# The gate of attention computed with seven products of sums, behind the pooled branch's product

## The chip, the core and the metric

The kernel runs on one core of a Trainium2 chip. A core has engines with instruction queues of their own: TensorE (PE, matrix products; PEld is its weight load), VectorE (DVE), ScalarE (ACT), GpSimd (POOL) and SyncE (SP, which here issues DMAs). They wait for each other by semaphores; each takes its instructions in the order in which they were recorded. The metric is the device time of one execution in microseconds (us), lower is better.

## The reference

Two layers of the same kind over T = 528 tokens (16 learned meta tokens and 512 of the input), width 1024. Cut to what matters here:

```python
h = rms_norm(x, norm_g)
q, k, v, gate_a, u_b, gate_b, q_idx, k_idx, w_idx, merge = split(h @ w_in)
score = einsum(relu(q_idx . k_idx), w_idx)        # per query, over visible keys
_, sel = top_k(score, 128)                        # 128 keys per query
attn = softmax_attention(q, k[sel], v[sel])       # 8 heads of 64
y_a = (attn * silu(gate_a)) @ w_a                 # gate_a: 512 columns
pooled = multiscale_pool(u_b, pool_w, pool_b, pool_s)
y_b = (pooled * silu(gate_b)) @ w_b
g_a, g_b = split(sigmoid(merge))                  # 2 x 1024 columns
out = x + (g_a * y_a + g_b * y_b) @ w_out
```

`k_top` is min(256, 512 // 4) = 128, so a query tile needs 16 rounds of "the eight largest, then strike them out".

## The kernel before

**Numbers.** Every matrix product is made of three of the fast format fp32r: each operand is split into a high part (rounded to fp32r) and a low part (what is left), and high x high, high x low and low x high are summed in PSUM. `hhi` and `hlo` are the parts of h, transposed: 8 blocks of 128 rows by 528 tokens.

**Weights.** All weights pass as a list of chunks of 128 x 2048 numbers, in the order of use (L112 to L124). `w_load` (L129) fetches a chunk into `raw` over SP's queue. `w_prep_enqueue` (L155) then puts the items of its preparation into `prep_q`, one chunk ahead of use. There are three kinds: plain (ACT makes the high part, DVE the low part), `by_dma` (ACT makes the high part and a negated copy, to which an accumulating DMA on POOL's queue adds the raw weights, L189 to L199), and `mixed` (L212 to L277). The mixed kind serves a scheme in which a 2 x 2 block product is made from seven products of sums of blocks instead of eight: nine items, in which ACT casts seven blocks and DVE makes seven low parts and five sums of weight blocks, each 128 x 512.

**The two ways to multiply.** `dense` (L495) computes 128 output columns for up to 512 tokens: 24 matmuls for 8 blocks of depth. `mix_gates` (L878) computes a chunk of 256 output columns for all tokens in two halves of `n2` (264 in layer 0, 256 in layer 1) as seven products of twelve matmuls, named "a11", "a12", "s2", "s1", "s3", "s4" and "a22". The sums of h that it needs (`hsum`) are made by `sums_of_h` (L806) during earlier stages, part of them by way of DRAM (`far`, `hsheet`). Three PSUM banks U, S and X change roles by chunk (`ROLES`, L875). `total` adds a partial result out of PSUM on DVE, `gate` applies tanh on ACT (sigmoid and silu are made of tanh). Ahead of a product the items of preparation that it needs are recorded (`NEEDS`), and after each product more of them, `LEAD` = 5 items ahead.

**The stages of a layer**, in PE's order: keys and index queries; the pooled branch's gate (dense); the pooled branch's input (dense); queries of heads 0 to 3; *the attention gate, two dense chunks, into* `sila`; queries of heads 4 to 7; y_b = the pooled branch's product with `w_b`, two chunks, into `zb`; the merge gates, eight chunks with `mix_gates`; y_a, the product with `w_a`; the output product.

**What is woven in between.** After each group of matmuls `group_done` (L320) runs work that is due, in this order: functions put off by `later`; an item of `prep_q`; steps of the generator at the head of `fill` (the attention), at `rate` steps per group, half of that in `half_done`; and steps of the top-k:

```python
spare[0] += FULL * (pe.us - seen[0]) - (dve.us - seen[1])
spare[0] = min(spare[0], CAP)
while spare[0] > 0 and sel:
    next(sel[0])                      # one step; its DVE cost is taken off spare
```

`pe.us` and `dve.us` are sums of costs that the code itself assigns to the instructions recorded so far (`pe_cost`, `dve_cost`, L71 and L80: a fp32r matmul costs n / 2167 us, a DVE operation 0.15 us and 0.00104 us a column). `topk_steps` (L635) serves two query tiles at once: a step is a pair of MAX8 or a pair of MATCH_REPLACE8, 16 rounds of two steps each. Query tiles 0 and 1 go first, then tiles 2 and 3, whose rows have 400 and 528 keys.

The attention (L657) goes through 16 units u of two heads (u // 4 is the query tile), with three steps each. In step one of unit u the logits of u + 1 and the scaling of u, in step two the softmax of u + 1 and the values of u - 1, in step three the transposes of u and, behind each tile, `gated` (L744): the tile's result times `sila`, in place. Before a tile's first logits, `ensure(i)` in `attend` (L1141) finishes the top-k that the tile needs: for tiles 0 and 1 the first generator, for tiles 2 and 3 both, recording all that is left at once. `splits` and `alos` then make the parts `ahi` and `alo` for y_a. The attention is put into `fill` ahead of y_b (L1153), at R_ATT = 1.95 (layer 0) and 1.7 (layer 1).

Of the kernel before, what the change touches and what calls it, by code (L numbers as in the profile page):

```python
# [26 lines left out]
HB = 272  # L27
NCOL = 968
LB = 6
R_ATT = (1.95, 1.7)  # L30
FULL = 1.0
CAP = 1.5
W0 = 3
# [54 lines left out]
def tile_block(ctx: ExitStack, tc: tile.TileContext, x, meta, w_in, pool_w, w_a, w_b, w_out, rows, hgain, c_tab, out):  # L88
# [24 lines left out]
    for l in range(2):  # L113
        wi = w_rows(w_in[l], 0, w_in.shape[2])
        chunks.append([(wi[:, :, 512:640], 0), (wi[:, :, 2688:2816], 128)])
        mb = [3784, 4040, 4296, 4552]
        order = [2176, 2432, 1664, 1920, 1408, 1152, 0, 640, 896, 256]
        chunks += [[(wi[:, :, c:c + 256], 0)] for c in order]
        chunks += [[(w_rows(w_b[l], c, 512), 0)] for c in (0, 512)]
        by_dma |= set(range(len(chunks) - 10, len(chunks)))  # L120
        mixed |= set(range(len(chunks), len(chunks) + 8))
        chunks += [[(wi[:, :, c:c + 256], 0)] for c in (*mb, 2760, 3016, 3272, 3528)]
        chunks += [[(w_rows(w_a[l], c, 512), 0)] for c in (0, 512)]
        chunks += [[(w_rows(w_out[l], c, 256), 0)] for c in (0, 256, 512, 768)]  # L124

# [171 lines left out]
    def later(fn, n=2):  # L297
        pend.append((count[0] + n, fn))
# [358 lines left out]
    def attention(ensure):  # L657
# [92 lines left out]
        for u in range(-1, 17):  # L750
            if u + 1 < 16:
                logits(u + 1)
            if 0 <= u < 16:
                scale(u)
            yield
            if u + 1 < 16:
                soft(u + 1)
            if u >= 1:
                values(u - 1)
                if u % 4 == 0:  # L760
                    meta_values(u // 4 - 1)
            yield
            if u >= 1 and u % 4 == 0:
                gated(u // 4 - 1)
            if 0 <= u < 16:
                turn(u)
                if u % 4 == 3:
                    meta_turn(u // 4)
            yield
# [36 lines left out]
    def sums_of_h(l, s0, n2):  # L806

        ts_ = one.tile([128, 2, 2, 4, T // 2], F32R, tag="R", name="hsum")
        c0, c1 = slice(s0, s0 + n2), slice(s0 + n2, s0 + 2 * n2)
        far = dram.tile([128, 2, 2, 2, n2], F32, name=f"far{l}")  # L810
        nf = NF[0]
        t1_ = []

        def sums(g):
            k = slice(2 * g, 2 * g + 2)
            a0, a1, b0, b1 = nf[0][:, k, c0], nf[0][:, k, c1], nf[1][:, k, c0], nf[1][:, k, c1]
            dve.tensor_tensor(a0, a1, a0, op=OP.subtract)
            dve.tensor_tensor(a1, b1, a1, op=OP.subtract)
            dve.tensor_tensor(b1, b1, a0, op=OP.subtract)
            dma(far[:, 0, g], a0)  # L820
            act.copy(ts_[:, 1, 0, k, :n2], a1)
            act.copy(ts_[:, 0, 0, k, :n2], b1)

        def lows(g):
            k = slice(2 * g, 2 * g + 2)
            a1, b0, b1 = nf[0][:, k, c1], nf[1][:, k, c0], nf[1][:, k, c1]
            dve.tensor_tensor(b0, b0, b1, op=OP.subtract)
            dma(far[:, 1, g], b0)
            dve.tensor_sub(ts_[:, 1, 1, k, :n2], a1, f(ts_[:, 1, 0, k, :n2]))
            dve.tensor_sub(ts_[:, 0, 1, k, :n2], b1, f(ts_[:, 0, 0, k, :n2]))  # L830

        back = {}

        def fetch(w, g):
            if (w, g) == (0, 1):
                back[w, g] = [(slice(k, k + 1), sheet(n2, "hsheet")[:, None, :n2]) for k in (2, 3)]
            else:
                t = tmp.tile([128, T], F32, tag="B", name="hsheet", bufs=8) if w == 0 else sheet(T, "hsheet")
                back[w, g] = [(slice(2 * g, 2 * g + 2), t[:, :2 * n2].rearrange("p (k c) -> p k c", k=2))]
            for k, t in back[w, g]:  # L840
                dma(t, far[:, w, g, k.start - 2 * g:k.stop - 2 * g])

        def high(w, g):
            if w == 0 and not t1_:
                t1_.append(one.tile([128, 2, 4, T // 2], F32R, tag="Alo", name="hsum1"))
            for k, t in back[w, g]:
                act.copy(H[0][:, k, c1] if w else t1_[0][:, 0, k, :n2], t)

        def low(w, g):
            for k, t in back.pop((w, g)):  # L850
                hi, lo = [H[s][:, k, c1] if w else t1_[0][:, s, k, :n2] for s in range(2)]
                dve.tensor_sub(lo, t, f(hi))

        early = deque([lambda: sums(0), lambda: lows(0), lambda: sums(1), lambda: lows(1)])
        late = deque([lambda: fetch(1, 0), lambda: fetch(1, 1), lambda: high(1, 0), lambda: low(1, 0),
                      lambda: high(1, 1), lambda: low(1, 1), lambda: fetch(0, 0), lambda: fetch(0, 1)])

        def last_sum():
            for g in range(2):
                high(0, g)  # L860
            for g in range(2):
                low(0, g)

        operands = {
            "a11": lambda s, k: H[s][:, k, c0],
            "a12": lambda s, k: H[s][:, 4 + k, c0],
            "s4": lambda s, k: H[s][:, 4 + k, c1],
            "s1": lambda s, k: t1_[0][:, s, k, :n2],
            "s2": lambda s, k: ts_[:, 0, s, k, :n2],
            "s3": lambda s, k: ts_[:, 1, s, k, :n2],  # L870
            "a22": lambda s, k: H[s][:, k, c1],
        }
        return early, late, last_sum, operands
# [1 line left out]
    ROLES = [(0, 1, 2), (2, 0, 1), (1, 2, 0)]  # L875
    NEEDS = {"a11": 1, "a12": 2, "s2": 4, "s1": 5, "s3": 6, "s4": 7, "a22": 8}

    def mix_gates(zb, ta, s0, n2, operands, splits, alos):  # L878
        base = popped[0] - progress[W["use"]]
        end_ = [None]  # L880
        for q in range(8):
            c = W["use"]
            W["use"] += 1
            ops = ready[c]
            w_prep_enqueue()
            bs = [bank("d") for _ in range(3)]
            U, S, X = (bs[r] for r in ROLES[q % 3])
            done = [0]

            def product(ps, name, start):  # L890
# [8 lines left out]
            def end():  # L899
                done[0] += 1  # L900
                group_done()
                while prep_q and (popped[0] < base + 9 * q + LEAD + done[0] * 9 // 7 or (q == 7 and done[0] > 4)):
                    prep_one()

            def gate(eh, t, src, in_sheet):
                j = 2 * q + eh
                cs = slice(s0 + t * n2, s0 + (t + 1) * n2)
                if q < 4:
                    th = src if in_sheet else sheet(n2, "th")[:, :n2]
                    act.activation(th, src, AF.Tanh, scale=0.5)  # L910
                    d = zb[:, j, cs]
                    later(lambda: dve.scalar_tensor_tensor(d, th, 1.0, d, op0=OP.add, op1=OP.mult), 2)
                else:
                    end_[0] = act.activation(ta[j - KT][:, cs], src, AF.Tanh, scale=0.5).ins

            def total(eh, t, ps, part):
                o = sheet(n2, "c")[:, :n2]
                dve.tensor_tensor(o, ps[:, :n2], part, op=OP.add)
                gate(eh, t, o, True)

# [30 lines left out]
            end()  # L951
            splits()
            ready.pop(c)
        return end_[0]


# [41 lines left out]
    for l in range(2):  # L998
# [124 lines left out]
        ta = {}  # L1123

        queries(0)
        sa = one.tile([128, 4, T], F32, tag="D", name="sila")
        SIL["a"] = sa
        for c in range(2):
            w = chunk()
            for mi in range(2):  # L1130
                j = 2 * c + mi
                for hf, a, n, o in halves:
                    ps = dense(w, mi, a, n)
                    th = sheet(n, "th")
                    act.activation(th[:, :n], ps[:, :n], AF.Tanh, scale=0.5)
                    later(lambda th=th, ps=ps, j=j, a=a, n=n: dve.scalar_tensor_tensor(
                        sa[:, j, a:a + n], th[:, :n], 1.0, ps[:, :n], op0=OP.add, op1=OP.mult), 1)
                    group_done()
        queries(1)

        def attend():  # L1141
            def ensure(i):
# [7 lines left out]
            if l == 0:  # L1150
                yield from meta_attn(qm)

        fill.append(attend())  # L1153
        rate[0] = R_ATT[l]
        for c in range(2):
            w = chunk()
            if c == 1:
                hold[0] = 5
            for mi in range(4):
                j = 4 * c + mi  # L1160
                for hf, a, n, o in halves:
                    ps = dense(w, mi, a, n, (mhi, mlo), 4)
                    act.copy(zb[:, j, a:a + n], ps[:, :n])  # L1163
                    if late and (l == 1 or hf):
                        late.popleft()()
                    group_done() if hf else half_done()
# [14 lines left out]
                a, n = alo_q.pop(0)  # L1181
                dve.tensor_sub(alo[:, :, a:a + n], sa[:, :, a:a + n], f(ahi[:, :, a:a + n]))

        gates_end = mix_gates(zb, ta, s0, n2, operands, splits, alos)
        drain()
        splits()
        alos()
# [147 lines left out]
```

## Time and profile before

| | us |
|---|---|
| median of 3 runs (lowest, highest) | 772.63 (771.91, 772.87) |
| the profiled execution | 774.25 |
| its span, first to last instruction | 772.5 |
| PE, DVE, ACT, POOL busy in the span | 754.8, 557.9, 475.0, 235.4 |
| mean granted PE clock | 0.991 of full speed |

A row of the profile names the source line (most have L60, the line of the helper that records PE's and DVE's instructions), the engine, the operation and the tiles as out<-in. In a group's row stand the count, the busy time in us, the mean duration in ns, and the idle time of the engine just before with what ended it. A matmul's own duration (about 290 ns) overlaps with those of its neighbours; what one costs PE is read from the time of a series. In a timeline and in the chain of waits the two first numbers are start and duration in us. A wait's row has the sum, the number of times and the longest.

### The profile page before, as it was taken

Reading aid. Unit: us, or ns where it says so; the run is one execution under the profiler, and the core shown is the slowest. Engines: PE = TensorE matmul, PEld = TensorE weight load, DVE = VectorE, ACT = ScalarE, POOL = GpSimd, SP = SyncE. Lnnn points to the kernel's source line nnn. Section 1 sums busy time; section 2 is a strip of 40 time slices with the busy share of each in tenths; the row PEclk is TensorE's granted clock in tenths of the full one; section 3 lists DMA queues with packets and bytes.
Section 4 is the critical chain, followed back from the end, with each engine's and each line's share of the span. In section 5 each row is a group of like instructions: output and inputs, shape, how many; then the busy total and the mean of one; then the engine's idle time right before and its main releaser. Section 6 shows DMA issues by size and latency. Waiting matters only on the chain.

```text
span 772.5 us, 15843 instructions
## 1 busy us (share of the span) xinstructions
PE 754.8 (98%) x5989; PEld 718.7 (93%) x5989; DVE 557.9 (72%) x1396; ACT 475.0 (61%) x1046; POOL 235.4 (30%) x304
## 2 busy tenths in 40 slices
PE   6999999999999999999999999999999999999998
PEld 5999999999999999999999988988979899999998
DVE  6856787888787786775357658868799887769531
ACT  5577754736788786534244787365668887864420
POOL 6552164425220110043345421652511221104300
PEclk8999999999999999999999999999999999999999
DMA  8538586586022111453513477858721221136311
GB/s 294 183 83 217 140 178 165 125 204 165 2 83 83 55 56 56 149 183 115 161 58 109 111 195 173 192 127 205 183 87 56 75 90 56 56 109 221 129 50 42
DMA packets 73549, 96.96 MB, mean 126 GB/s; under 512 B 3664, under 2 KB 58736, under 8 KB 73472
## 3 DMA queue, kind: packets, MB, share of 16 engines
q1 hardware_dynamic: 67712, 74.97, 30.5%
q0 software_dynamic: 5760, 20.97, 14.8%
q8 instruction: 47, 0.77, 0.4%
q14 instruction: 30, 0.25, 0.1%
HBM read 66.41 MB, written 8.55 MB: 97 GB/s over the span
## 4 chain that ended last, share of the span: by engine, by line
PE 82%; DVE 9%; ACT 5%; POOL 1%; issue 1%; DMA 1%; SPq 0%; DVEq 0%; ACTq 0%; POOLq 0%
PE d L60 67%; PE a L60 11%; PE v L60 4%; DVE w L60 2%; DVE nf L60 1%; ACT lt L691 1%; DVE hlo L60 1%; ACT w L222 1%; DVE t L60 1%; DVE sc L60 1%; DMA hsheet<-far 1%; DVE alo L60 0%; DMA xt<-in_x_dram 0%; DVE raw L60 0%; DVE m L60 0%
## 5 line engine op out<-in xcount | busy, mean ns | idle before, releaser
L60 PE MATMUL d<-hhi,w 128*128 128x256 f32 (+3 forms) x1408 | 289.8, 297 | 0.0
L60 PEld LDWEIGHTS d<-hhi,w 128*128 128x128 f32 x1408 | 226.3, 188 | 7.0 <-issue 1.6
L60 PE MATMUL d<-hlo,w 128*128 128x256 f32 (+3 forms) x704 | 193.6, 294 | 0.6 <-POOL hlo L1202 0.6
L60 PE MATMUL d<-w,hhi 128*128 128x256 f32 (+2 forms) x928 | 145.8, 286 | 2.0 <-DVE w L60 0.9
L60 PEld LDWEIGHTS d<-hlo,w 128*128 128x128 f32 x704 | 132.5, 188 | 3.3 <-POOL hlo L1202 0.8
L60 PEld LDWEIGHTS d<-w,hhi 128*128 128x128 f32 (+1 forms) x928 | 125.8, 187 | 6.4 <-ACT hhi L462 2.2
L60 DVE TENSOR_TENSOR w<-raw,w 128x512 fp32r<-128x512 f32 (+1 forms) x130 | 110.0, 857 | 2.2 <-ACT w L222 2.1
L703 POOL TENSOR_SCALAR pm<-lt,rs 128x16 f32<-128x16 f32 x64 | 40.3, 644 | 183.1 <-DVE rs L60 169.2
L60 PE MATMUL d<-w,hlo 128*128 128x256 f32 (+2 forms) x464 | 85.2, 282 | 0.0
L60 PE MATMUL d<-hsum,w 128*128 128x264 f32 (+1 forms) x576 | 77.8, 286 | 0.0
L60 PEld LDWEIGHTS d<-hsum,w 128*128 128x128 f32 x576 | 72.0, 188 | 1.5 <-issue 0.7
L60 PEld LDWEIGHTS d<-w,hlo 128*128 128x128 f32 (+1 forms) x464 | 68.0, 187 | 0.4
L192 POOL DMA_DIRECT2D w<-raw x40 | 36.4, 925 | 104.0 <-ACT w L191 83.4
L222 ACT CAST w<-raw 128x512 fp32r<-128x512 f32 x96 | 56.3, 623 | 2.9 <-DVE raw L60 2.9
L1202 POOL TENSOR_TENSOR hlo<-ta,hhi 128x256 fp32r<-128x256 f32 (+1 forms) x32 | 31.1, 988 | 82.0 <-ACT hhi L1201 82.0
L60 DVE MATCH_REPLACE8 sc<-m,sc 128x400 f32<-128x400 f32 (+2 forms) x100 | 54.3, 548 | 0.0
L60 DVE MAX8 m<-sc 128x8 f32<-128x400 f32 (+2 forms) x100 | 52.7, 556 | 0.8
L691 ACT ACTIVATE lt<-lt,mn,NR 128x144 f32<-128x144 f32 (+3 forms) x64 | 42.4, 665 | 12.0 <-DVE mn L60 12.0
L60 PE MATMUL d<-mhi,w 128*128 128x272 f32 (+2 forms) x192 | 48.9, 331 | 0.4 <-ACT zb L1163 0.4
L191 ACT ACTIVATE w<-raw 128x1024 fp32r<-128x1024 f32 x40 | 41.3, 1057 | 11.3 <-PE d L60 11.3
L60 DVE SCALAR_TENSOR_TENSOR sc<-r,wsg,sc 128x144 f32<-128x144 f32 (+3 forms) x56 | 32.4, 581 | 15.5 <-ACT r L615 13.2
L580 POOL TENSOR_TENSOR t<-t,t 128x256 f32<-128x256 f32 (+1 forms) x34 | 30.8, 907 | 39.2 <-DVE t L60 39.2
(199 smaller groups left out, 1372.4 us busy)
## 6 DMA issues: line engine op xcount, KB each, us to landing
raw<-in_w_in_dram SPq DMA_DIRECT2D x72, 512.0 KB, 3.9
w<-raw POOLq DMA_DIRECT2D x40, 512.0 KB, 5.9
raw<-in_w_out_dram SPq DMA_DIRECT2D x16, 512.0 KB, 3.4
kept<-res SPq DMA_DIRECT2D x16, 264.0 KB, 2.5
res<-kept SPq DMA_DIRECT2D x16, 264.0 KB, 6.5
raw<-in_w_branch_b_dram SPq DMA_DIRECT2D x8, 512.0 KB, 4.4
raw<-in_w_branch_a_dram SPq DMA_DIRECT2D x8, 512.0 KB, 3.5
xt<-in_x_dram SPq DMA_DIRECT2D x4, 512.0 KB, 5.3
```

The source lines that it names most:

```text
L60: return fn(*a, **k)
L191: act.activation(t, raws[c][s], AF.Copy, scale=-1.0)
L192: gp.dma_start(t, raws[c][s], accum_op=OP.add)
L222: act.copy(t[:, 0], blk[src[n]])
L580: gp.tensor_tensor(t1[:m, :256], t1[:m, :256], t2[:m, :256], op=OP.add)
L691: act.activation(L[hh][:, :n], L[hh][:, :n], AF.Exp, scale=NR[:, i, h:h + 1], bias=mn[:, hh:hh + 1], accum_out=sm[:, hh:hh + 1])
L703: gp.tensor_scalar(pms[i][:, 2 * j + hh, :], L[hh][:, 0:16], rs[:, hh:hh + 1], None, op0=OP.mult)
L1202: gp.tensor_sub(hlo[:, j, a:a + n], d, f(hhi[:, j, a:a + n]))
```

## The change

The attention gate's two chunks (columns 640 and 896 of `w_in`) are taken out of the dense stages and put ahead of the merge gates in `mix_gates`, whose loop now runs over q = -2 to 7. The results go to `sila`; the formula is the same (tanh of the half, plus one, times the value). In `chunks` they leave `by_dma` for `mixed`. Queries of heads 4 to 7 follow directly on those of heads 0 to 3. The attention is put into `fill` one chunk later, ahead of y_b's second chunk, with R_ATT = 1.55 and 1.4, and waits before the third step of unit 4, which is the first to use `sila`, until both gate chunks are done (`SIL["ready"]`). One buffer of `hsheet` moves from tag "B" to tag "L" of the pool `tmp`.

```diff
-R_ATT = (1.95, 1.7)
+R_ATT = (1.55, 1.4)
...
-        order = [2176, 2432, 1664, 1920, 1408, 1152, 0, 640, 896, 256]
+        order = [2176, 2432, 1664, 1920, 1408, 1152, 0, 256]
...
-        by_dma |= set(range(len(chunks) - 10, len(chunks)))
-        mixed |= set(range(len(chunks), len(chunks) + 8))
-        chunks += [[(wi[:, :, c:c + 256], 0)] for c in (*mb, 2760, 3016, 3272, 3528)]
+        by_dma |= set(range(len(chunks) - 8, len(chunks)))
+        mixed |= set(range(len(chunks), len(chunks) + 10))
+        chunks += [[(wi[:, :, c:c + 256], 0)] for c in (640, 896, *mb, 2760, 3016, 3272, 3528)]
...
             yield
+            while u == 4 and not SIL["ready"]:
+                yield
             if u >= 1 and u % 4 == 0:
                 gated(u // 4 - 1)
...
-                t = tmp.tile([128, T], F32, tag="B", name="hsheet", bufs=8) if w == 0 else sheet(T, "hsheet")
+                t = sheet(T, "hsheet")
...
-    def mix_gates(zb, ta, s0, n2, operands, splits, alos):
+    def mix_gates(sa, zb, ta, s0, n2, operands, splits, alos):
...
-        for q in range(8):
+        for q in range(-2, 8):
...
-            U, S, X = (bs[r] for r in ROLES[q % 3])
+            U, S, X = (bs[r] for r in ROLES[(q + 2) % 3])
...
-                while prep_q and (popped[0] < base + 9 * q + LEAD + done[0] * 9 // 7 or (q == 7 and done[0] > 4)):
+                while prep_q and (popped[0] < base + 9 * (q + 2) + LEAD + done[0] * 9 // 7 or (q == 7 and done[0] > 4)):
...
-                if q < 4:
+                if q < 0:
+                    th = sheet(n2, "th")[:, :n2]
+                    act.activation(th, src, AF.Tanh, scale=0.5)
+                    d = sa[:, j + 4, cs]
+                    later(lambda: dve.scalar_tensor_tensor(d, th, 1.0, src, op0=OP.add, op1=OP.mult), 1)
+                elif q < 4:
...
-                o = sheet(n2, "c")[:, :n2]
+                cs = slice(s0 + t * n2, s0 + (t + 1) * n2)
+                o = sa[:, 2 * q + eh + 4, cs] if q < 0 else sheet(n2, "c")[:, :n2]
...
             ready.pop(c)
+            SIL["ready"] = q >= -1
...
         queries(0)
+        queries(1)
         sa = one.tile([128, 4, T], F32, tag="D", name="sila")
         SIL["a"] = sa
-        for c in range(2):
-            w = chunk()
-            for mi in range(2):
-                j = 2 * c + mi
-                for hf, a, n, o in halves:
-                    ps = dense(w, mi, a, n)
-                    th = sheet(n, "th")
-                    act.activation(th[:, :n], ps[:, :n], AF.Tanh, scale=0.5)
-                    later(lambda th=th, ps=ps, j=j, a=a, n=n: dve.scalar_tensor_tensor(
-                        sa[:, j, a:a + n], th[:, :n], 1.0, ps[:, :n], op0=OP.add, op1=OP.mult), 1)
-                    group_done()
-        queries(1)
+        SIL["ready"] = False
...
-        fill.append(attend())
         rate[0] = R_ATT[l]
         for c in range(2):
             w = chunk()
             if c == 1:
                 hold[0] = 5
+                fill.append(attend())
```

More of the change, by code (lines that the diff above doesn't have):

```diff
@@ L1182, in alos @@
                 dve.tensor_sub(alo[:, :, a:a + n], sa[:, :, a:a + n], f(ahi[:, :, a:a + n]))
-        gates_end = mix_gates(zb, ta, s0, n2, operands, splits, alos)
+        gates_end = mix_gates(sa, zb, ta, s0, n2, operands, splits, alos)
         drain()
```

## The prediction

> **What bounds the kernel now.** I read the page's busy line first, then the waits of PE over the whole span, then each engine's share by stretch.
>
> ```profile
> PE 754.8 (98%) x5989; PEld 718.7 (93%) x5989; DVE 557.9 (72%) x1396; ACT 475.0 (61%) x1046; POOL 235.4 (30%) x304
> ```
> ```profile
> PE v L60 <- ACT hhi L462: 2.4, 3, 1.1
> PE d L60 <- DVE alo L60: 2.1, 2, 1.8
> ```
> ```profile
> 139.30:163.30 24.00, 24.00 (x202) 24.00 (x202) 22.65 (x62) 13.06 (x22) 6.49 (x7) 1.00 0.74 177
> ...
> 191.00:326.30 135.30, 133.77 (x1138) 127.54 (x1137) 102.68 (x268) 104.29 (x256) 18.29 (x30) 1.00 0.21 66
> ```
>
> PE is the bound: busy 754.8 of 772.5 us, and its two longest waits, summed by releaser, are 2.4 and 2.1 us. The windows' columns are the busy time of PE, PEld, DVE, ACT and POOL, the PE clock, the DMA share and GB/s. The first window is the attention gate's two chunks in layer 0, the second runs from the start of y_b to the end of the merge gates. Less work on PE is therefore worth its full time, as long as DVE keeps up; and under the attention gate DVE was busy 22.65 of 24.00 us. The next view keeps only DVE's work on the top-k maxima (MAX8, MATCH_REPLACE8 and its load), for the attention gate's stretch of either layer.
>
> ```profile
> 139.30:163.30 24.00, 17.06 (x44) 1.00 0.74 177
> ...
> 521.00:543.60 22.60, 13.80 (x36) 1.00 0.89 202
> ```
>
> So the dense gate was the cover of the top-k of query tiles 2 and 3: 17.06 us of it in layer 0, 13.80 us in layer 1.
>
> **PE work removed and added.** The chain of waits shows what a group costs on PE.
>
> ```profile
> 139.33 3.08 PE d L60 x24
> ...
> 142.70 2.92 PE d L60 x24
> ...
> 203.27 0.50 PE a L60 x4
> 203.77 1.43 PE d L60 x12
> 205.20 0.37 PE v L60 x4
> ...
> 258.69 1.46 PE d L60 x12
> ...
> 524.25 2.85 PE d L60 x12
> ...
> 583.00 1.61 PE d L60 x12
> ```
>
> Layer 0 loses four groups of 272 columns and four of 256: 4 x 3.08 + 4 x 2.92 = 24.0 us. Layer 1 loses eight times twelve matmuls of 512 columns: 8 x 2.85 = 22.8 us. Each layer gets 14 products of twelve matmuls: with 264 columns 14 x 1.45 = 20.3 us, with 256 columns (half of 2.85) 14 x 1.42 = 19.9 us. PE saves 3.7 + 2.9 = **6.6 us**. Some products of the mix take 1.61 us, so up to 28 x 0.16 = 4.5 us could be given back; I take 0 and keep 4.5 for the range.
>
> **Weights and sums.** Two chunks per layer leave the route of ACT casts and an accumulating DMA for the mixed one: 12 DVE operations of 512 columns each (7 low parts, 5 sums), and each product chunk has three additions out of PSUM.
>
> ```profile
> L60 DVE TENSOR_TENSOR w<-raw,w 128x512 fp32r<-128x512 f32 x96 | 64.8, 683 | 2.2 <-ACT w L222 2.1
> ...
> L60 DVE TENSOR_TENSOR c<-d,p 128x264 f32<-128x264 f32 x16 | 6.9, 430 | 16.4 <-PE d L60 12.5 <-ACT lt L691 2.2 <-ACT lt L702 1.5
> ```
>
> That is 24 x 0.683 + 6 x 0.43 = 19 us more DVE work per layer, none of it removed elsewhere, beside 20 us more of PE in the same stretch. Over a whole stretch it fits: DVE had 32.6 us of room there (135.30 - 102.68) and gets 20 us of PE time more. Price as an average: 0. The second row says also that DVE, when it reaches an addition, mostly stands waiting for PE (12.5 of 16.4 us idle): it is not behind when the burst below begins. The four accumulating DMAs per layer that go from POOL's queue, the moved loads on SP's queue and ACT's three small copies per chunk lie under a PE that is busy 133.77 of 135.30 us in this stretch: 0 each; the waits quoted name no DMA, and a late load would show there first.
>
> **Where the top-k goes.** This is the main term. A top-k step is issued only while the code's credit is positive: PE's metered cost less DVE's (L331 to L341). In the mix a chunk meters 84 x 264 / 2167 = 10.2 us for PE and, at 12 x 0.68 + 7 x 0.425, 11.1 us for DVE, the attention not counted; the credit has no floor, goes negative, and no step runs. Before, about 15 of the 32 instruction pairs that make up the top-k of tiles 2 and 3 ran under layer 0's dense gate (the 44 above, less a load for each replacement), and the rest beside queries and y_b. In the instruction list of the changed kernel 5 pairs of layer 0 stand ahead of y_b, 14 in it, none beside products 1 to 24; then `ensure(2)` (attention step 25, forced by logits of tile 2, after product 25) empties the generator at once: **13 pairs, 26 instructions in a row on DVE**. In layer 1 it is 5, 12, and then **15 pairs, 30 instructions**, after product 28. What a pair costs back to back, here under the dense gate, and what ends the top-k:
>
> ```profile
> 159.22 1.18 DVE L60 MAX8 m<-sc 128x8 f32<-128x400 f32 x2
> 160.32 0.07 DVE L60 MATCH_VALUE_LOAD sc<-m,sc 128x8 f32 x1
> 160.38 0.56 DVE L60 MATCH_REPLACE8 sc<-m,sc 128x400 f32<-128x400 f32 x1
> 160.86 0.08 DVE L60 MATCH_VALUE_LOAD sc<-m,sc 128x8 f32 x1
> 160.93 0.69 DVE L60 MATCH_REPLACE8 sc<-m,sc 128x528 f32<-128x528 f32 x1
> 161.53 0.43 DVE L60 SCALAR_TENSOR_TENSOR sila<-th,d 128x272 f32<-128x272 f32 x1
> ...
> 208.35 0.70 DVE L60 TENSOR_SCALAR sc<-sc 128x400 f32<-128x400 f32 x2
> ```
>
> A pair of maxima takes 160.32 - 159.22 = 1.10 us, a pair of replacements 161.53 - 160.32 = 1.21 us. Layer 0: 7 x 1.21 + 6 x 1.10 + 0.70 = 15.8 us. Layer 1: 8 x 1.21 + 7 x 1.10 + 0.70 = 18.1 us.
>
> What is queued behind it on DVE: the reciprocal with which the last exponentials are scaled, the low parts of the next weights, the additions that free PSUM. Who waits for that: in layer 0 PE's transposes of tile 1's last pair of heads, which need the scaled exponentials; in layer 1 the product "s2" of the next chunk, which needs its low part. DVE cannot start early either: the last addition before the burst waits for product 23 of PE in layer 0, for product 27 in layer 1. Between that and the wall PE has in layer 0 three products, four matmuls of logits, four of values and four transposes: 3 x 1.45 + 0.50 + 0.37 + 0.50 = 5.7 us; in layer 1 three products, logits, values and two matmuls: 4.3 + 0.50 + 0.37 + 0.24 = 5.4 us. (The logits are of 400 columns; the quoted four are shorter, so 0.2 us more is possible.)
>
> ```profile
> L60 DVE RECIPROCAL rs<-sm 128x2 f32<-128x2 f32 x32 | 5.1, 160 | 9.1 <-ACT lt L691 9.1
> ...
> L702 ACT ACTIVATE lt<-lt,rs 128x256 f32<-128x256 f32 x16 | 7.2, 501 | 0.8 <-DVE rs L60 0.8
> ```
>
> DVE's side in layer 0: addition 0.43, a low part 0.68, burst 15.8, two small operations 0.3, then two scalings on ACT 1.0: 18.2 us, less 5.7: **12.5 us** of PE stall. Layer 1: 0.43 + 18.1 + 0.3 + a low part 0.68 = 19.5, less 5.4: **14.1 us**. Bounds: 11 and 12.5 us if operations in a row overlap more than the rows show; 14 and 16 us if DVE enters the burst up to 2 us late.
>
> **After the stall.** DVE then holds the work that piled up behind the burst, and PE runs for some products at DVE's pace. The trace shows besides what the clock does after an idle PE, at the end of layer 0's merge gates.
>
> ```profile
> 328.00:330.00 2.00, 0.71 (x5) 0.72 (x6) 1.23 (x4) 0.42 (x1) 0.00 (x0) 0.95 0.96 297
> 330.00:332.00 2.00, 2.00 (x11) 2.00 (x11) 0.88 (x2) 0.42 (x1) 0.34 (x1) 0.50 1.03 350
> 332.00:334.00 2.00, 2.00 (x14) 2.00 (x14) 0.85 (x2) 0.32 (x1) 0.42 (x1) 0.70 1.05 407
> ```
> ```profile
> 329.29 0.89 PE L60 MATMUL d<-alo,w 128*128 128x272 f32 x4 [1.85 <-DVE alo L60]
> 329.97 1.91 PE L60 MATMUL d<-ahi,w 128*128 128x256 f32 x8
> 331.68 1.05 PE L60 MATMUL d<-alo,w 128*128 128x256 f32 x4
> 332.53 1.47 PE L60 MATMUL d<-ahi,w 128*128 128x272 f32 x8
> ...
> 334.33 1.11 PE L60 MATMUL d<-ahi,w 128*128 128x256 f32 x8
> ```
>
> After 1.85 us idle the granted clock was 0.50 and 0.70 for about 4 us, and the twelve 256-column matmuls from 329.97 to 332.53 took 2.56 us where twelve take 1.42: some 1.6 us lost with the neighbours. I charge 2.0 us per layer for both effects, 0 if the slow PE only fills DVE's arrears, 3.5 if they add. [...]
>
> **The end of the stage.** In layer 1 the last attention step now falls after the last product, so tile 3 is multiplied, cast and split there.
>
> ```profile
> 696.96 1.29 DVE L60 TENSOR_TENSOR alo<-sila,ahi 128x512 fp32r<-128x512 f32 x2
> 698.16 0.42 DVE L60 TENSOR_TENSOR c<-d,u 128x256 f32<-128x256 f32 x1
> 698.50 1.28 DVE L60 TENSOR_TENSOR alo<-sila,ahi 128x512 fp32r<-128x512 f32 x2
> ```
>
> The second low part that y_a's first group needs moves from ahead of that addition to behind it and behind the multiplication (0.68 us): 1.0 us later. In layer 0 only the 16 meta columns come late: 0.3 us. Together 1.3 us; 0 to 3 for the range.
>
> **Sum.** The profiled execution took 774.25 us, 1.75 around its span of 772.5. 774.25 - 6.6 + 12.5 + 14.1 + 4.0 + 1.3 = 799.6 us; it lay 1.6 us over the median of 772.63, so **798 us**.
>
> **Rivals.**
> *The burst is covered* (faster): PE has enough ahead to run through it. Then 772.63 - 6.6 + 1.3 = 767.3 us. For it: PE busy 133.77 of 135.30 us in the old stretch. Against it: the top-k lay mostly ahead of that stretch, and PE would need 16 us of work between two points that hold 5.7. It decides from there: a burst under 5.7 us costs nothing.
> *DVE never recovers* (slower still): the arrears, at most the 5.7 us that PE ran ahead, delay exponentials and weights up to the end of the attention, and each chunk waits anew. 5 us per layer more, 808 us. Against it: averaged over the stretch DVE has room.
> *The products save nothing*: at 1.61 us they give back 4.5 us: 802 us; a handful in the old mix are so long, most are 1.43 to 1.46.
>
> **How the numbers follow.** Forecast 0.85, never recovers 0.07, products save nothing 0.04, covered 0.04. The low end takes the low bounds (stalls 23.5, arrears 1, tail 0.5: 772.63 - 6.6 + 25 = 791), a little lower for overlap: 789; the high end 772.63 - 6.6 + 30 + 7 + 3 = 806. A time within 0.2% of before is as good as no change here; no case lands there but by cancellation: 0.01. Faster 0.04, slower 0.95.
>
> **What would show it.** In the profile after: about 6.6 us less PE work; on DVE a run of 26 and one of 30 top-k instructions with nothing between; PE idle 12 to 14 us during each, the transposes in layer 0 and a product on "hsum" in layer 1 behind it; a granted clock near half just after; no stall of that size elsewhere. I am wrong if PE works through the burst, or if its stalls lie elsewhere, as in y_b, where DVE also has little room.

## The result, and the profile after

The changed kernel takes **800.73 us** (median of 4 runs, 800.17 to 801.9) against 772.75 for the kernel before (4 runs on the same chip): ratio 1.0352, 95% interval 1.0332 to 1.0373. It is slower by 28 us; 798 was predicted. The profiled execution took 800.17 us with a span of 798.4, so the span grew by 25.9.

From the page after, PE's and DVE's busy time:

```profile
PE 751.4 (94%) x6037; PEld 719.3 (90%) x6037; DVE 590.9 (74%) x1456; ACT 479.5 (60%) x1074; POOL 225.3 (28%) x296
```

PE was busy 98% of the span and is now 94%. DVE has 33.0 us more to do (590.9 - 557.9), 16.5 per layer. The waits of PE after (sum, times, longest):

```profile
PE d L60 <- DVE w L60: 16.9, 4, 15.2
PE a L60 <- ACT lt L702: 12.2, 1, 12.2
PE d L60 <- DVE sila L60: 2.3, 2, 1.2
...
PE d L60 <- DVE alo L60: 1.3, 1, 1.3
```

Before, no sum was above 2.4 us. Two single waits, 12.2 and 15.2 us, come to 27.4 us, more than the span grew; all the rest together is a gain of 1.5. The timeline of DVE after, around the first and then the second of them:

```profile
228.00 0.42 DVE L60 TENSOR_TENSOR c<-d,p 128x264 f32<-128x264 f32 x1
228.34 0.68 DVE L60 TENSOR_TENSOR w<-raw,w 128x512 fp32r<-128x512 f32 x1
228.94 0.08 DVE L60 MATCH_VALUE_LOAD sc<-m,sc 128x8 f32 x1
...
244.01 0.70 DVE L60 TENSOR_SCALAR sc<-sc 128x400 f32<-128x400 f32 x2
...
244.70 0.15 DVE L60 RECIPROCAL rs<-sm 128x2 f32<-128x2 f32 x1
...
620.54 0.42 DVE L60 TENSOR_TENSOR c<-d,u 128x256 f32<-128x256 f32 x1
620.87 0.08 DVE L60 MATCH_VALUE_LOAD sc<-m,sc 128x8 f32 x1
...
638.24 0.70 DVE L60 TENSOR_SCALAR sc<-sc 128x400 f32<-128x400 f32 x2
...
639.00 0.67 DVE L60 TENSOR_TENSOR w<-s,w 128x512 fp32r<-128x512 f32 x1
```

and the timeline of PE after for the same two places (in brackets the idle time before the group and what ended it):

```profile
231.56 1.72 PE L60 MATMUL d<-hsum,w 128*128 128x264 f32 x12
245.51 1.30 PE L60 MATMUL a<-consts,lt 128*128 128x128 f32 x4 [12.22 <-ACT lt L702]
...
624.10 0.40 PE L60 MATMUL d<-hsum,w 128*128 128x256 f32 x2
639.72 2.50 PE L60 MATMUL d<-hsum,w 128*128 128x256 f32 x10 [15.23 <-DVE w L60]
```

This is the burst of the prediction: an addition, in layer 0 one low part, then only top-k from 228.94 to 244.6 us and from 620.87 to 638.8 us. Behind it stand the reciprocal (whose scaling on ACT PE's transposes wait for) and, in layer 1, the low part of a product that PE had begun with two matmuls. The stretches after the stalls, from the windows after (busy PE, PEld, DVE, ACT, POOL, then the granted clock, DMA share and GB/s):

```profile
236.00:240.00 4.00, 0.00 (x0) 0.00 (x0) 4.00 (x11) 0.00 (x0) 0.00 (x0) 0.56 0.01 2
...
246.00:248.00 2.00, 2.00 (x10) 2.00 (x11) 1.93 (x8) 1.15 (x3) 0.28 (x1) 0.50 0.48 94
248.00:250.00 2.00, 2.00 (x11) 2.00 (x11) 1.29 (x3) 1.32 (x5) 0.00 (x0) 0.50 0.48 168
250.00:252.00 2.00, 2.00 (x16) 2.00 (x16) 2.00 (x6) 0.97 (x3) 0.00 (x0) 0.98 0.00 0
...
640.00:642.00 2.00, 2.00 (x10) 2.00 (x11) 2.00 (x7) 1.78 (x5) 2.00 (x2) 0.50 0.00 0
642.00:644.00 2.00, 2.00 (x17) 2.00 (x16) 1.97 (x8) 1.99 (x5) 0.04 (x1) 0.84 0.00 0
```

PE comes back at half clock: a 2 us window holds 10 or 11 matmuls where 16 or 17 are normal. Last, the chain of waits after, in the stretch with the gate's products (start, duration):

```profile
203.93 1.47 PE d L60 x12
...
210.31 1.46 PE d L60 x12
...
577.98 0.69 DVE w L60
...
590.95 0.42 DVE sila L60
...
595.82 1.68 PE d L60 x12
...
602.25 1.42 PE d L60 x12
```

The products cost what was taken for them, 1.46 and 1.42 us, with some at 1.6 to 1.7. But in layer 1 the chain runs through DVE and ACT, not PE, from 578 to 596 us: DVE set the pace there 25 us before the burst. From 596 us to the last addition but one ahead of it, at 616.73, the chain is PE's again.

### The profile page after: what moved, and what is told of

It reads as the page before. It is cut to its first block, busy times and chain, and to the rows that moved or that the text cites. A ratio compares the mean times of both kernels' runs of the same rounds, so it can differ in the third digit from the quotient of the medians.

```text
span 798.4 us, 16004 instructions
## 1 busy us (share of the span) xinstructions
PE 751.4 (94%) x6037; PEld 719.3 (90%) x6037; DVE 590.9 (74%) x1456; ACT 479.5 (60%) x1074; POOL 225.3 (28%) x296
## 4 chain that ended last, share of the span: by engine, by line
PE 80%; DVE 13%; ACT 4%; issue 1%; POOL 1%; DMA 1%; SPq 0%; DVEq 0%; ACTq 0%; POOLq 0%
PE d L60 64%; PE a L60 11%; PE v L60 4%; DVE w L60 3%; DVE sc L60 2%; DVE m L60 2%; DVE nf L60 1%; ACT w L222 1%; DVE raw L60 1%; DVE hlo L60 1%; DMA xt<-in_x_dram 1%; ACT lt L691 1%; DVE ta L60 0%; DVE s L60 0%; DVE sila L60 0%
## 5 line engine op out<-in xcount | busy, mean ns | idle before, releaser
L60 PE MATMUL d<-hhi,w 128*128 128x256 f32 (+3 forms) x1344 | 272.0, 293 | 2.3 <-DVE sila L60 2.3
L60 PEld LDWEIGHTS d<-hhi,w 128*128 128x128 f32 x1344 | 216.4, 190 | 7.5 <-DVE sila L60 3.0
L60 PE MATMUL d<-hlo,w 128*128 128x256 f32 (+3 forms) x672 | 184.0, 290 | 0.6 <-POOL hlo L1201 0.6
L60 DVE TENSOR_TENSOR w<-raw,w 128x512 fp32r<-128x512 f32 (+1 forms) x154 | 126.7, 834 | 4.2 <-ACT w L222 3.9
L60 PE MATMUL d<-hsum,w 128*128 128x264 f32 (+1 forms) x720 | 98.9, 289 | 16.3 <-DVE w L60 16.0
L60 PEld LDWEIGHTS d<-hsum,w 128*128 128x128 f32 x720 | 90.8, 191 | 19.3 <-DVE w L60 16.6
L222 ACT CAST w<-raw 128x512 fp32r<-128x512 f32 x120 | 70.4, 622 | 6.3 <-DVE raw L60 5.6
L702 ACT ACTIVATE lt<-lt,rs 128x128 f32<-128x128 f32 (+3 forms) x64 | 32.5, 556 | 39.2 <-DVE rs L60 39.2
L192 POOL DMA_DIRECT2D w<-raw x32 | 29.3, 943 | 70.5 <-ACT w L191 49.1
L60 DVE SCALAR_TENSOR_TENSOR sc<-r,wsg,sc 128x144 f32<-128x144 f32 (+3 forms) x56 | 32.4, 582 | 14.5 <-ACT r L615 12.3
L615 ACT ACTIVATE r<-a,wab 128x272 f32<-128x272 f32 (+2 forms) x80 | 35.5, 493 | 8.9 <-PE a L60 8.9
```

What stands on the lines that cost most here:

```text
L60: return fn(*a, **k)
L192: gp.dma_start(t, raws[c][s], accum_op=OP.add)
L222: act.copy(t[:, 0], blk[src[n]])
L615: act.activation(r[:, n - 1::-1] if i == 0 else r[:, o:o + e], ps[:, :e], AF.Relu, scale=wab[:, i, h:h + 1])
L702: act.activation(L[hh][:, 16:n], L[hh][:, 16:n], AF.Copy, scale=rs[:, hh:hh + 1])
```

## The experiments

Times are medians; the kernel before, run beside them, took 772.7 to 774.8 us. The ratio in brackets is against it, with its 95% interval. The first question was whether the burst is the cause and enough of a cause; the second, what the change costs apart from it.

**The burst left out.** In `topk_steps` the rounds for tiles 2 and 3 end where they stand when `ensure` comes to them.

```diff
+    cut = [False]
...
+            if cut[0] and tiles[0]:
+                break
...
+                cut[0] = i >= 2
...
+                cut[0] = False
```

> The changed kernel without the top-k pairs that are still left when tile 2's logits come (13 pairs in layer 0, 15 in layer 1): tiles 2 and 3 select too few keys, everything else is as in the changed kernel. Theory (the two bursts are the loss): both stalls of 12.2 and 15.2 us go, and with them the half clock behind them, some 2 us each; 800.7 - 27.4 - 4 = 769 us, 766 to 773, faster than before. Rival A (DVE's 19 us per layer of added weight preparation are the loss): nothing of the 28 us comes back but what 33 us less DVE work gives by chance; 790 or more. Rival B (the late start of the attention and its lower rate are the loss): 790 or more.

769.24 us (0.9944, 0.9927 to 0.9962). PE's waits:

```profile
PE d L60 <- DVE sila L60: 2.3, 2, 1.2
...
PE d L60 <- DVE w L60: 1.6, 3, 0.9
```

Both long waits are gone, and with them 31.5 us. What the products save is then there: PE is busy for 748.4 us, 6.4 less than before, and the span is 767.7 us, 4.8 less than before (by the medians the gain is 4.2 us). Without this top-k work the change would pay. The kernel leaves the work out, though, and does not only break up its run; whether the change pays with the work done elsewhere is asked further down.

**The burst alone, in the kernel before.** The gate stays dense and in its place; only the top-k may not run under it.

```diff
-        while spare[0] > 0 and sel:
+        while spare[0] > 0 and sel and not shut[0]:
...
         SIL["a"] = sa
+        shut[0] = True
...
+        shut[0] = False
         queries(1)
```

> The kernel before with top-k steps shut out only while the dense attention gate runs. Its dense gate, its weight preparation and its attention rate stay as they were; 28 top-k instructions (14 pairs) are then left at the forced point in layer 0 and 26 (13 pairs) in layer 1. Theory: stalls of about 16.9 - 5.7 = 11 and 15.8 - 5.4 = 10 us and 2 us behind each: 772.7 + 25 = 798 us, 788 to 806, so the whole loss without any part of the new scheme. Rival A and B: DVE lacks the added preparation and the attention starts as early as before, so the burst is mostly covered: under 780.

804.83 us (1.0402, 1.038 to 1.0425). PE's largest wait:

```profile
PE a L60 <- ACT lt L703: 26.2, 2, 13.2
```

The same wait for the scaled exponentials, once per layer, with no product of sums added for the gate and the gate in its old place. Taking away the cover is enough. The two stalls are 13 us each, where 11 and 10 were expected, so the time lies at the upper end of the expected range.

**Place alone.** The gate stays dense but stands behind y_b, with the attention and `SIL["ready"]` as in the changed kernel; by then part of the second half of the tokens in h has been overwritten by sums, so the gate's values differ.

```diff
+        chunks += [[(wi[:, :, c:c + 256], 0)] for c in (640, 896)]
+        by_dma |= set(range(len(chunks) - 10, len(chunks)))
+        mixed |= set(range(len(chunks), len(chunks) + 8))
...
-        for q in range(-2, 8):
+        for q in range(8):
...
+        for c in range(2):
+            w = chunk()
...
+                    ps = dense(w, mi, a, n)
```

> The place alone: the attention gate stands behind y_b as in the changed kernel, the attention starts and runs at the changed kernel's rates, but the gate's two chunks are still dense and prepared by the accumulating DMA. PE work is that of the kernel before. Theory (what is lost is DVE's room ahead of the forced point, not the place): by the instruction list the credit lets all of the top-k run beside y_b and the dense gate, no run of more than 8 is left; 771 to 778 us. Rival B (the late start and the lower rate of the attention are the loss): 790 or more.

774.25 us (1.0015, 1.0 to 1.003), with PE's largest wait

```profile
PE d L60 <- DVE w L60: 4.4, 3, 1.8
```

A dense gate covers the top-k of tiles 2 and 3 as well behind y_b as ahead of it. So it is not the move that harms; what is left is that the products bring DVE work of their own and so cover less.

**The stall filled.** 50 matmuls of 512 columns, whose result nobody reads, stand on PE ahead of tile 2's first logits.

```diff
                 ensure(i)
+                if i == 2:
+                    ps = bank("a")
+                    for _ in range(50):
+                        pe.matmul(ps[:, :512], hhi[:, 0, 0:128], hhi[:, 0, 0:512], start=True, stop=True)
```

> The changed kernel with 50 matmuls of 512 columns that nothing reads (50 x 0.232 = 11.6 us) ahead of tile 2's first logits, so that PE is busy during most of both stalls of 12.2 and 15.2 us and its clock is not lowered. If the half clock behind the stalls costs what its 4 to 6 us of slow matmuls lose: 800.7 - 2 x 2 = 797 us, 794 to 799. If DVE's arrears hide the slow PE: 800 to 802. If the added matmuls delay the path (they should end ahead of the top-k): over 803.

798.19 us (1.0318, 1.0293 to 1.0344), 2.5 less than the changed kernel (a rough size, since the intervals of the two kernels overlap), with a mean clock of 0.993 instead of 0.979. The longest wait that is left stands in layer 1:

```profile
PE d L60 <- DVE w L60: 5.5, 4, 3.9
```

The windows behind the two places (columns as above):

```profile
246.00:250.00 4.00, 4.00 (x32) 3.92 (x31) 3.57 (x11) 2.48 (x7) 0.02 (x1) 1.00 0.50 135
...
638.00:642.00 4.00, 4.00 (x23) 3.68 (x22) 3.96 (x12) 3.30 (x9) 2.01 (x2) 0.61 0.00 0
```

In layer 0 the half clock is gone. In layer 1, where PE still stood idle for 3.9 us, it is not. Comparing the two traces matmul by matmul, this kernel is 0.25 us ahead of the changed one when PE starts again at 245.5 us, 2.0 us ahead from 251 us on, and 1.7 us ahead behind the second place. So the half clock behind the first stall costs 1.75 us; what it costs behind the second was not taken away here. The rest of the loss is DVE's time, whatever PE does meanwhile.

**All work kept, the top-k earlier.** Now the theory that DVE has room on average: a greater credit leaves no burst.

```diff
-FULL = 1.0
+FULL = 1.3
```

> The changed kernel with one constant changed: the credit's factor FULL is 1.3 instead of 1.0, so that more of the top-k is recorded ahead of the merge stage and none is left at the forced point. All work is there. Theory: no run of more than 8 top-k instructions in the merge stage, no PE wait over 3 us there, 768 to 772 us. Rival A (added weight preparation): DVE has the same work as in the changed kernel, so 790 or more. Rival C (DVE has no room anywhere, so that the top-k only moves its stall forward to the queries and the pooled branch's product): the long stalls go, but as much appears there; 785 or more.

789.73 us (1.0207, 1.0183 to 1.023): the theory missed by 18 us, and the figure of the rival by which the top-k takes its stall along (785 or more) was the right one. PE's waits:

```profile
PE a L60 <- DVE qs L60: 12.6, 13, 2.0
PE d L60 <- DVE sila L60: 4.6, 5, 1.4
PE d L60 <- DVE w L60: 3.7, 5, 1.7
```

No wait is over 2.0 us, but there are many, and most lie in the query stages (`qs`), into which the top-k was moved. Whether they belong to the change or to the factor was tried on the kernel before.

**The same factor in the kernel before.** The edit is the same line.

> The kernel before, its top-k credit growing 1.3 times as fast as PE's meter and nothing else changed: a control for the changed kernel with the same factor, whose largest wait (12.6 us in 13 waits of PE for the split queries, longest 2.0) lies in the query stages and not in the mix. By the instruction list 16 more top-k instructions stand ahead of the pooled branch's product in layer 0 and 20 more in layer 1 than in the kernel before. Theory: moving the top-k ahead costs by itself, since the query stages have no room on DVE with or without the change; PE waits for the split queries here too, 4 to 12 us in all, and the time is 776 to 784 us; then most of what the factor cost in the changed kernel belongs to the remedy. Rival: with the dense gate between the two query stages the same factor is free, under 1 us of new waits and 772 to 774 us; then those waits belong to the change, which took the gate out from between the queries.

781.67 us (1.0089, 1.0072 to 1.0106). PE's largest wait:

```profile
PE a L60 <- DVE qs L60: 7.8, 8, 1.7
```

The theory of the control was right: most of the `qs` waits belong to the factor. With the factor in both kernels the change still costs 789.73 - 781.67 = 8 us (9 by the ratios), where the products alone would save 6.6. So there are some 15 us of loss that are no burst, 4.8 of them further waits for `qs` (12.6 - 7.8).

**All work kept, the top-k spread over the mix**, 0.55 steps per product, on top of the credit.

```diff
+                tick[0] += 0.55
+                while tick[0] >= 1:
+                    tick[0] -= 1
+                    if sel:
+                        next(sel[0])
```

> The changed kernel with a top-k step recorded after every second product of the merge stage (0.55 steps per product), so that the same 13 and 15 pairs stand beside products 1 to 25 and 1 to 29 instead of in one run behind them. Theory: what counts is not only that the run is in one piece but that DVE has no room ahead of the forced point. By the rows' durations DVE has there 59 us of work in layer 0 and 72 in layer 1, PE 50 and 60; PE can be behind by the 5.7 and 5.4 us that it ran ahead; so stalls of about 3.5 and 6.5 us stay, in many small waits: 779 us, 774 to 785. If only the run in one piece were to blame: 770 or less. Rival A: 790 or more.

789.48 us (1.0206, 1.0186 to 1.0226), 10 us over what was expected, though the query stages are as in the changed kernel:

```profile
PE d L60 <- DVE sila L60: 10.8, 7, 2.6
PE d L60 <- DVE c L60: 4.7, 4, 2.2
```

PE now waits for PSUM banks that DVE's additions empty late. These two orders win back 11 of the 28 us and no more; the theory of room on average fell. The new one: the stretch from y_b to the end of the mix has no room on DVE for the top-k *and* the preparation of the gate's chunks.

**The preparation left out**, the low parts and the sums of the gate's two chunks. The question was whether the gate's DVE work takes the room, or the lost cover alone.

```diff
+            if gatec:
+                return
...
-            eng.tensor_tensor(blk[to], blk[x], blk[y], op=op)
+            if not gatec:
+                eng.tensor_tensor(blk[to], blk[x], blk[y], op=op)
```

> The changed kernel with the DVE work of the two gate chunks' preparation left out (seven low parts and four sums of 512 columns per chunk, 2 x 11 x 0.683 = 15 us per layer, so DVE's additions out of PSUM, top-k and attention stay); the gate's products use the high part where the low one stood, as many and as long as before, and the gate's values are less exact or wrong. The code's credit then lets more top-k steps run: by the instruction list 6 pairs' worth less than half the burst stays (6 instructions at the wall in layer 0, 8 in layer 1: 3.5 and 4.9 us). My theory: the room on DVE that this preparation takes is what the change lacks, so without it the products' saving comes out whole and the short bursts lie under PE's 5.7 and 5.4 us: 769 us (766 to 772). Rival: the lack is not the preparation but the lost cover of the dense gate (17 and 14 us of top-k in the stretch where attention and additions stand already): stalls of 1 to 4 us stay all over the mix as in the kernels where the top-k was spread, 780 us or more.

770.38 us (0.9961, 0.9948 to 0.9973). PE's largest wait:

```profile
PE d L60 <- DVE w L60: 3.4, 2, 2.5
```

Only 22 operations per layer are gone, 44 of 1456. But that does not tell the two causes apart: without their preparation the products become a cover themselves. From 187 to 212 us, under layer 0's gate products, DVE's work on the top-k maxima was

```profile
187.00:212.00 25.00, 8.75 (x21) 1.00 0.23 65
```

where the changed kernel has none in the same window and the dense gate behind y_b has 12.14 us. What the two kernels with work left out do show is the sum: leaving out either load, the rest of the top-k or the preparation, gives 769 or 770 us; with both, all on DVE, the kernel is at 789 to 801.

**Sums of weights on POOL.** To make room without dropping work, two of a chunk's four sums go to POOL, with the attention starting with the mix at higher rates and FULL = 1.1; then all four.

```diff
-            mix(dve, "a21", "a21", "a22", OP.add)
+            mix(gp, "a21", "a21", "a22", OP.add)
...
-            mix(dve, "a12", "a12", "s2", OP.subtract)
+            mix(gp, "a12", "a12", "s2", OP.subtract)
```

> The changed kernel with room made for DVE, all work kept: two of the four sums of each mixed chunk go to POOL (1.24 us less on DVE per chunk), the attention starts with the merge stage at rates 1.75 and 1.55 (the forced point comes 4 to 5 products later), and the credit's factor is 1.1. At most 6 top-k instructions are left at the forced point. Theory: DVE's work up to the forced point fits under PE's but for 2 to 4 us per layer; 770 us, 767 to 777. Rival C (the top-k cannot be hidden at all without the dense gate): 785 or more.

> As the run with room made for DVE, but all four sums of a mixed chunk are on POOL. A sum of 512 columns there costs about 1.9 us (twice the 0.99 us that its 256-column subtraction took in the kernel before), four of them 7.6 us per chunk of 12 us, and three of them are in a chain, so a product may wait for weights. Theory: DVE has 1.2 us more room per chunk: 768 us, 766 to 774, unless the chain on POOL shows as waits of PE on weights; then 775 to 785.

791.75 us (1.0249, 1.0217 to 1.0281) with two, 810.46 us (1.0484, 1.0463 to 1.0505) with four: far off the theory. The first of them changes several things at once, so its time can't be put down to POOL alone. The second differs from the first in nothing but two more sums on POOL, and these cost 18.7 us. The groups between 190 and 350 us show DVE's operations beside POOL's sums. The changed kernel:

```profile
L60 DVE TENSOR_TENSOR raw<-raw 128x512 f32<-128x512 f32 x18 | 12.4, 688 | 0.3
L60 DVE TENSOR_TENSOR raw<-raw,s 128x512 f32<-128x512 f32 x9 | 6.2, 684 | 0.0
L60 DVE TENSOR_TENSOR s<-raw 128x512 f32<-128x512 f32 x9 | 6.2, 684 | 0.0
L60 DVE TENSOR_TENSOR w<-s,w 128x512 fp32r<-128x512 f32 x9 | 6.1, 682 | 0.1
...
L60 DVE TENSOR_TENSOR mn<-mn,RQ 128x2 f32<-128x2 f32 x13 | 2.1, 161 | 0.5
```

The same view with two sums on POOL:

```profile
L228 POOL TENSOR_TENSOR raw<-raw 128x512 f32<-128x512 f32 x9 | 12.3, 1362 | 32.3 <-issue 28.6 <-DVE raw L60 3.6
...
L60 DVE TENSOR_TENSOR s<-raw 128x512 f32<-128x512 f32 x9 | 8.3, 922 | 0.0
...
L60 DVE TENSOR_TENSOR mn<-mn,RQ 128x2 f32<-128x2 f32 x15 | 5.5, 366 | 0.5
```

and with four:

```profile
L60 DVE TENSOR_TENSOR w<-s,w 128x512 fp32r<-128x512 f32 x9 | 9.1, 1016 | 2.6 <-ACT w L222 2.6
```

POOL takes 1362 ns where DVE takes 688, and the means of DVE's own operations grow beside it: 684 to 922, 161 to 366 and, with four sums, 682 to 1016 ns. The mean hides that most of them are as short as ever. With two sums on POOL, the same stretch (shortest, median and longest in ns):

```profile
L60 DVE TENSOR_TENSOR s<-raw x9: 676/679/1773, 195.7 to 321.9; 128x512 f32<-128x512 f32 x9
```

Only the two of these nine that ran while POOL was making a sum took 1.77 us. And DVE still gets less to do: its busy time falls from 590.9 us to 583.6 and, with four sums, 571.2. So the time is not lost by more work on DVE. With four, ACT's casts wait for POOL's sums, here in ACT's waits of that stretch, and PE's largest wait over the whole span is for ACT's copies out of PSUM (`p`, 11.0 us in 8 waits), which share ACT's queue with the casts:

```profile
ACT w L222 <- POOL s L228: 22.3, 6, 4.7
```

**Half the change.** One gate chunk (640) dense in its old place, the other (896) as products; then the same with the attention starting with the mix at 1.95 and 1.75 steps per group.

```diff
-R_ATT = (1.55, 1.4)
-FULL = 1.0
+R_ATT = (1.7, 1.55)
+FULL = 1.1
...
-        for q in range(-2, 8):
+        for q in range(-1, 8):
...
+        for c in range(1):
+            w = chunk()
...
+                    ps = dense(w, mi, a, n)
```

> One of the two gate chunks (columns 640) stays dense in its old place between the two query stages, the other (896) goes as seven products ahead of the merge gates; the top-k's credit grows 1.10 times as fast as PE's meter, and the attention is started at 1.7 and 1.55 steps per group. Half the preparation (8.8 us of DVE per layer), half the products' saving (3.3 us), half the cover kept (12 us of PE per layer under which the top-k runs); no burst is left by the instruction list. My theory: DVE has room for half the change, so the time is 772.7 - 3.3 + 1 to 2 us of small waits: 771 us (768 to 774). Rival: DVE has no room to give at all beside the mix, every us of work added to the stretch comes back as a wait: half of what the spread kernels lost against 766, so 776 to 780 us.

> As the kernel before it, but the attention starts only with the first chunk of products instead of beside the pooled branch's second chunk, at 1.95 and 1.75 steps per group, so that more of the top-k lies beside the pooled branch's product and the attention is denser in the mix. Theory: the same total work on DVE, so the same time within 3 us of that kernel, 771 to 776 us. Rival: the denser attention makes exponentials late, as where the attention stood at 1.95 beside the top-k: 780 us or more.

777.23 us (1.0055, 1.0037 to 1.0072) and 781.58 us (1.0109, 1.009 to 1.0127): the rivals had the right figures both times. Largest waits for DVE or ACT in the first

```profile
PE a L60 <- DVE qs L60: 3.7, 4, 1.3
```

and in the second, beside the same 3.7 us,

```profile
PE a L60 <- ACT lt L702: 3.2, 3, 1.8
```

Part of this loss may belong to FULL = 1.1, which the control shows to be costly at 1.3; the two were not taken apart. No kernel that does all the work beat the kernel before.

## Why the prediction was right

The predicted time was 798 us and the measured one 800.7. Term by term, against the span (the predicted terms add up to 25.3 us, measured 25.9):

| step | predicted | measured |
|---|---|---|
| stall in layer 0 | 12.5 | 12.2 |
| stall in layer 1 | 14.1 | 15.2 |
| after the stalls | 4.0 | 3.3 (798.4 - 767.7 with and without the burst, less 27.4) |
| all else (products -6.6, end of stage 1.3) | -5.3 | -4.8 (span without the burst, 767.7 - 772.5) |

**The burst.** Place, length and the two waiting instructions came out as predicted: 15.7 us (228.94 to 244.63) for 15.8, and 18.0 (620.87 to 638.85) for 18.1. That it makes the two long stalls is shown by leaving its work out and by making it alone in the kernel before.

**PE's lead.** In layer 0 PE worked 5.3 us between the start of DVE's last addition (228.00) and its own stop (245.51 - 12.22 = 233.29); 5.7 was taken. In layer 1 it was 3.9 us (620.54 to 624.49) for 5.4. Both additions came late. The trace has the products that they wait for ended at 226.94 and 618.48, so DVE was 1.1 and 2.1 us late, and from these ends PE worked for 6.3 and 6.0 us, some 0.6 more than was taken. In layer 0 the two nearly cancel, which is luck; in layer 1 they do not, which is why this stall is 1.1 us longer than predicted. The prediction had read from the kernel before that DVE mostly stands waiting for PE at its additions, and kept "up to 2 us late" for the range. It is so at the addition before this one, where DVE waited 0.43 us for PE:

```profile
616.73 0.42 DVE L60 TENSOR_TENSOR c<-d,p 128x256 f32<-128x256 f32 x1 [0.43 <-PE d L60]
```

But from there to 620.54 six operations follow without a pause, five of them low parts and sums of weights: the preparation stands ahead of the next addition in DVE's queue.

**After the stalls.** 3.3 us for 4.0. The filled stall puts 1.75 on the half clock behind the first stall; as much behind the second would be 3.5, an estimate, and would explain all of it. The charge of 2.0 per layer was the author's estimate, made from the 1.6 us that PE lost behind 1.85 us of idle in the trace of before, and was meant for two effects, the clock and the work piled up on DVE. Of the second the runs show nothing, so that its size came out near is in part luck.

**The products** cost 1.46 and 1.42 us as taken, so the rival in which they save nothing is out; PE's busy time without the top-k's rest, 6.4 us less than before, says the same. (In the page after it is only 3.4 us less, where the matmuls at half clock are in it.) **The end of the stage** was charged 1.3 us that do not show: PE's wait for `alo` fell from 2.1 to 1.3 us. In its place came 2.3 us of waits for `sila` in layer 1, which were not foreseen: a gate product waits for a bank that DVE has not emptied yet.

**An error of count.** The prediction (and the part ahead of it) gives a mixed chunk five sums of weights. It is four: in the groups above stand 18 + 9 + 9 sums to 9 chunks (one `w<-s,w` each). So the added DVE work is 22 x 0.683 + 6 x 0.43 = 17.6 us per layer, not 19. The page shows 16.5: it counts time in which the durations of two operations overlap once, and sums of weights that are shown with 0.68 us start 0.60 us apart (619.33, 619.93, 620.54 in the timeline of DVE after).

**The step that did not hold** is the one that priced this work at 0 "as an average". In the sum it did no harm, since the top-k gave way to it and the whole lack came out as the burst. But as a statement about the stage it is wrong: with the top-k moved or spread the lack comes back as many short waits (789 us either way), and of what was tried only dropping the preparation or the rest of the top-k ends it (770, 769). The prediction saw the form that the lack took, and not that it would take another form if this one were barred. That a burst shorter than PE's lead costs nothing was borne out in part: of the two short bursts in the kernel without preparation (3.5 and 4.9 us by its instructions) the one in layer 0 left no wait over 0.7 us in the mix, while layer 1 had one of 2.5 us.

What stays open: what the half clock costs behind the second stall, how the 15 us that are no burst divide between DVE's length of work and its order in the queue, and whether half the change with the old credit would come to the time of before.

## What to carry to other kernels

When a change trades work of the bound engine for work on a second one, add up the second one's work over the stretch *with* what was hidden under the removed work: here 3 us of PE per layer were bought with 16.5 us of DVE, in a stretch that also lost the cover of 14 to 17 us of top-k. An issue rule that lets work wait until "there is room" doesn't make it vanish; look for the point that forces what is left, and count the instructions that are due there. To see whether order or room is lacking, drop each load once: if dropping either one mends it and reordering doesn't, it is room.

## What the runs showed of the hardware

Beside a sum on POOL some of DVE's own operations took longer. With two sums per chunk on POOL, between 190 and 350 us, seven of nine 512-column sums on DVE took 676 to 686 ns and the two that ran while POOL was making a sum 1.77 us; of fifteen two-column ones, nine took 160 ns and the six beside a sum on POOL 409 to 961 ns. Not every DVE operation beside a sum was longer: three low parts took 677 to 684 ns as ever. On POOL 9 sums as `raw<-raw` alone took 12.3 us, and four sums of each chunk there instead of two made the kernel 18.7 us slower.

In the first stall the clock was down to 0.56 in the window that begins 2.7 us after PE stopped, and stayed at one half until about 4.5 us after PE came back at 245.51 (0.50 up to 250, 0.98 from there). With PE kept busy until 3.9 us before the second restart, it was 0.61 in the window 638 to 642 us.
